# A hybrid mixer and FFN block on one core: the tile of split x is moved by 32 bytes in SBUF

## Chip, cores and metric

The kernel runs on one core of one Trainium2 chip. The time is the device time of one execution in microseconds. Three runs of the kernel before took 1726.85, 1731.55 and 1733.17 us; the median is 1731.55.

## What is computed

One layer of a post-norm trunk, for 256 tokens of 2048 channels, all in float32. `reference.py`, cut down:

```python
def reference(x, ...):
    mix = token_mixing(x, ...)
    x = layer_norm(DEEPNORM_ALPHA * x + mix, ln1_g, ln1_b)
    ffn = conv_ffn(x, ffn_w_up, ffn_conv_w, ffn_conv_b, ffn_w_down)
    return layer_norm(DEEPNORM_ALPHA * x + ffn, ln2_g, ln2_b)

def token_mixing(x, ...):
    proj = x @ w_in + b_in
    fox_qkv, fox_f, sgu_uv, gdn_qkv, gdn_a, gdn_b, gdn_gate, gates = jnp.split(proj, ...)
    y_a = forgetting_attention(fq, fk, fv, jax.nn.log_sigmoid(fox_f))
    y_b = spatial_gating(su, sv, ...)
    y_c = gdn_mixer(gdn_qkv, gdn_a, gdn_b, gdn_gate, ...)
    gt = jax.nn.sigmoid(gates).reshape(bsz, s, N_BRANCH, D_MODEL)
    merged = (gt[:, :, 0] * (y_a @ w_proj_a) + gt[:, :, 1] * (y_b @ w_proj_b)
              + gt[:, :, 2] * (y_c @ w_proj_c))
    return merged @ w_out

def conv_ffn(x, w_up, conv_w, conv_b, w_down):
    h = causal_depthwise_conv(x @ w_up, conv_w) + conv_b
    h_gate, h_val = jnp.split(h, 2, axis=-1)
    return (jax.nn.silu(h_gate) * h_val) @ w_down
```

`w_in` has 2048 x 15384 elements, `w_up` 2048 x 11008, `w_down` 5504 x 2048.

## The kernel before

Nearly all of the work is products of activations with weights that are read once from memory. To keep float32 accuracy with the fast operand type fp32r, each operand is split in a high part (the value rounded to fp32r, written by ACT at L114) and a low part (the rest, by DVE at L115). A product is then three: high times high, high times low, low times high.

`wload` (L117) brings a piece of weights of 512 KB into a tile `raw` by a DMA on SP's queue and splits it into `wh` and `wl`, each [128, 1024]. Four buffers of each rotate. Two functions use them:

- `stream_a` (L128) makes outputs of [128 tokens, 512 channels] for both blocks of tokens. The activations are the resident operand (loaded into the array, 128 x 128), the weights run through with 512 columns. Three products for each block of 128 rows of weights and each block of tokens: L134 (high, high), L135 (high activations, low weights), L136 (low activations, high weights).
- `stream_b` (L162) makes outputs of [128 channels, 256 tokens]. The weights are the resident operand and the activations run through. High and low part of the activations lie side by side in one row of 512 columns, so L178 does two of the three products at once with 512 columns, and L179 the third with the high part alone, 256 columns. For the last block of rows the order of the two is turned (L181, L182).

`stream_b_halves` (L186) is a variant for the first piece of the FFN: it goes block by block of tokens, and each product runs two separate runs of 128 columns through the array (L199, L200).

The tile of activations in `stream_b` is `xhl` (L235) in the first half of the program and `x1hl` (L958) in the FFN: 128 partitions, 16 blocks of 128 channels, each block a row of 512 columns, 256 tokens of the high part and 256 of the low part. Both are one buffer of the pool `hl`. `xhl` is filled at the start from x by `load_x` (transposes on PE at L243, then the split); `x1hl` is filled from the normed result of the mixers by `x1_turn` (L985). The streams of the input projection that make token rows (values, gates) use `xhl` in `stream_a`, through `xh` and `xl` (L256, L259), as the resident operand. The other products of `stream_a` use tiles from other pools: the mixers' outputs (`yah`, `ybh`, `ych` and their low parts), the merged result (`mh`, `ml`) and the FFN's hidden values (`aH`, `aL`).

The order of the program: the gated delta rule's q, k, v by `stream_b` (0 to about 170 us), the attention's q and k by `stream_b` and its values by `stream_a`, the spatial gate's two halves, twelve pieces of gates and branch projections by `stream_a` (to about 880 us), the output projection, layer norm 1, and the FFN in three groups of hidden blocks (16, 16 and 11), each with `stream_b` up and `stream_a` down. The small work of the mixers (attention, delta rule, gating) is cut into steps that generators yield; `tick` (L100) runs one step between two blocks of weights. A list scheduler sets the order within each engine.

Pools are laid out one behind the other in SBUF in the order in which they are opened: const, small, `wraw` (`raw`), `wspl` (`wh`, `wl`), `hl`, `resp` (x, the merged result, the residual), `wk`, then the mixers' slots or the FFN's tiles. Each tile starts at a multiple of 32 bytes. `raw`, `wh`, `wl`, the tile of `hl`, and the large tiles behind it all start 32 bytes past a multiple of 64. Of the tiles that are operands of PE, the constants `ident`, `utri` and `ones` start at a multiple of 64.

Of the kernel before, what the change touches and what calls it, by code (L numbers as in the profile page):

```python
# [44 lines left out]
def trunk_kernel(ctx, tc, x, w_in, b_in, sgu_ln_g, sgu_ln_b, sgu_w, sgu_b, gdn_conv_w, gdn_a_log,  # L45
# [39 lines left out]

# [1 line left out]
    ident = const.tile([P, P], F32, name="ident")  # L87
# [8 lines left out]

# [1 line left out]
    queue = []  # L98

    def tick():  # L100
        """One step of the oldest pending piece of work, between two steps of a weight stream."""
        while queue:
            try:
                next(queue[0])
                return
            except StopIteration:
                queue.pop(0)
# [9 lines left out]
    def wload(src, k0, nk, c0, n, dst=None, low=nc.vector, ahead=150):  # L117
        """Weight rows k0*128.. (nk blocks), columns c0..c0+n: list over blocks of (high, low) views."""
        with tc.high_priority(offset=ahead):
            raw = wraw.tile([P, 1024], F32, tag="raw", name=nm("raw"))  # L120
            rv = raw[:, 0:nk * n].rearrange("p (k n) -> p k n", n=n)
            nc.sync.dma_start(rv, src[k0 * P:(k0 + nk) * P, c0:c0 + n].rearrange("(k p) n -> p k n", p=P))
            hh, ll = dst or (wspl.tile([P, 1024], F32R, tag="wh", name=nm("wh")),
                             wspl.tile([P, 1024], F32R, tag="wl", name=nm("wl")))
            split(hh[:, 0:nk * n], ll[:, 0:nk * n], raw[:, 0:nk * n], low)
        return [(hh[:, j * n:(j + 1) * n], ll[:, j * n:(j + 1) * n]) for j in range(nk)]

    def stream_a(src, nkb, c0, lh, ll, k_off=0, tail=0, spare=(), spare_last=False, done=None, pre=None):  # L128
        """[tokens, 512] outputs for both token blocks; the last tail k blocks go block by block of tokens."""
        accs = [acc(), acc()]  # L130
# [31 lines left out]
    def stream_b(src, c0, n, act, pre=None):  # L162
        """n//128 blocks of [128 channels, (main 256 | low part 256)]."""
        nb = n // P
# [21 lines left out]
    def stream_b_halves(src, c0, act):  # L186
        """As stream_b for 2 blocks, the tokens block by block: [128 channels, (main 2 x 128 | low part 2 x 128)]."""
        accs = [acc() for _ in range(2)]
        ws = []
        for k0 in range(0, KB, 4):  # L190
            ws += wload(src, k0, 4, c0, 256, low=nc.gpsimd)
        av = act.rearrange("p k (u t) -> p k u t", u=2)
        for tb in range(2):
            ts = slice(tb * P, (tb + 1) * P)
            for kb, w in enumerate(ws):
                for i in range(2):
                    a = accs[i].rearrange("p (u t) -> p u t", u=2)[:, :, ts]
                    cs = slice(i * P, (i + 1) * P)
                    nc.tensor.matmul(a, w[0][:, cs], av[:, kb, :, ts], start=kb == 0, stop=False)  # L199
                    nc.tensor.matmul(a, w[1][:, cs], av[:, kb, :, ts], start=False, stop=kb == KB - 1)  # L200
        return accs
# [4 lines left out]
    def rsqrt(dst, src, n):  # L206
        """dst = src ** -0.5 for positive normal src, by Newton steps."""
        t = sm(n)
# [6 lines left out]
    def rsqrt_column(dst, src):  # L215
        """The same for one column; the steps y <- y (y^2 src - 3) leave powers of two to the end."""
        t = sm(1)
# [6 lines left out]
    def rows_to_cols(src_rows, nr, name):  # L224
        """DRAM rows [nr, 128] -> SBUF [128, nr]."""
        r = wk.tile([P, 512], F32, tag="wk", name=nm("rows"))
# [6 lines left out]

# [1 line left out]
    xhl = hl.tile([P, KB, 2 * S], F32R, tag="hl", name="xhl")  # L235

    def transpose_split(dst_h, dst_l, src, kbs):
        """src(kb, tb) [128 tok, 128] -> dst_h/dst_l (kbs) for two blocks at a time."""
        p = mx()
# [21 lines left out]

# [1 line left out]
    mixers = ExitStack()  # L263
# [16 lines left out]
    def small_columns():  # L280
        """Forget gates, decays and betas: cumulative sums by rows, by columns and spread over partitions."""
        wsm = wraw.tile([P, 1024], F32, tag="raw", name="wsm")
        wsv = wsm[:, 0:KB * 24].rearrange("p (k n) -> p k n", n=24)
        nc.sync.dma_start(wsv[:, :, 0:8], w_in[:, O_FF:O_FF + 8].rearrange("(k p) n -> p k n", p=P))
        nc.sync.dma_start(wsv[:, :, 8:24], w_in[:, O_GA:O_GA + 16].rearrange("(k p) n -> p k n", p=P))
        # 24 high and 24 low columns side by side
        wst = wspl.tile([P, 1024], F32R, tag="wh", name="wst")[:, 0:KB * 48].rearrange("p (k u n) -> p k u n", u=2, n=24)
        split(wst[:, :, 0, :], wst[:, :, 1, :], wsv)
        # columns of w_in: 8 forget gates, 8 decays, 8 betas
        bsm = const.tile([48, 1], F32, name="bsm")  # L290
# [32 lines left out]
        nc.scalar.activation(g.beta, pv2[:, :, 16:24], AF.Sigmoid)  # L323
        # softplus(z) = max(z, 0) + log1p(exp(-|z|)); z = -f for the forget gates, a + dt for the decays
        z = const.tile([P, 2, 16], F32, name="z")
# [10 lines left out]
        nc.scalar.activation(e, zn, AF.Exp)  # L336
        # log1p(e) = 2 atanh(e / (2 + e))
        r = col32("r")
# [17 lines left out]
        for _ in range(8):  # L356
            yield
        # rows [16, 256] (forget: whole sequence; decay: per 128 tokens)
        ps = mx()
# [18 lines left out]

# [1 line left out]
    def inv_norm(ss, name):  # L380
        """1 / norm [128 tokens, 2, 8] from sums of squares [128, 16]."""
        nc.vector.tensor_scalar_add(ss, ss, RMS_EPS)
        rn = const.tile([P, 16], F32, name=name)
        rsqrt(rn, ss, 16)
        return rn.rearrange("p (t h) -> p t h", t=2)
# [7 lines left out]
    def gdn_decays():  # L393
        gnat, gbc = g.gnat, g.gbc
        # decays: dt[j, i] = exp(gc_i - gc_j), i >= j;  am[i, j] = exp(gc_i - gc_j), i > j
        dt_ = g.dt = slot("dt").rearrange("p (t h e) -> p t h e", t=2, h=H)
# [8 lines left out]
        for tb in range(2):  # L405
# [5 lines left out]
            yield  # L411
        # decay to the end of the first block
        g.el = const.tile([P, 8], F32, name="el")
# [3 lines left out]
        nc.scalar.activation(g.fw, gnat[:, 1, :], AF.Exp)  # L417
        # decayed queries of the second block: their factors
        nc.scalar.activation(gbc[:, :, P:S], gbc[:, :, P:S], AF.Exp)

    def gdn_keys():
# [17 lines left out]
        nc.vector.tensor_mul(fa, g.fv, rk)  # L439
        # row factor of k @ S in the second block: fa * exp(gc)  # L440
        nc.vector.tensor_mul(g.fw, g.fw, fa[:, 1, :])
        for tb in range(2):
            nc.gpsimd.tensor_mul(am[:, tb], am[:, tb], fa[:, tb, :, None].to_broadcast([P, H, P]))
        yield
        # inverse of (I + am): 32x32 diagonal blocks by elimination, one block per partition
        amv = g.amv = am.rearrange("p t h e -> p (t h) e")
# [22 lines left out]
    def gdn_inverse():  # L469
        amv, td = g.amv, g.td  # L470
        # keys by tokens, first block
        for q in range(2):
# [17 lines left out]
        yield  # L490
        # 32 -> 64
        pm = const.tile([P, 2, 32], F32, name="pm")
# [14 lines left out]
        for q in range(2):  # L507
# [8 lines left out]
            yield  # L516
        # of T itself only the first 64 are needed
        p8 = mx().rearrange("p (m e) -> p m e", e=32)
# [3 lines left out]
        yield  # L522
        # 64 -> 128 (transposed inverse only)
        p2s = []
# [53 lines left out]
    def gdn_blocks():  # L578
# [45 lines left out]
        for q, qs, hs in pair:  # L624
# [5 lines left out]
            yield  # L630
        # tot = rqs * rsqrt(rqs^2 * mean(oraw^2) + eps), rqs = rq / sqrt(head_dim)
        ssq = const.tile([P, 16], F32, name="ssq")
# [16 lines left out]

# [1 line left out]
    yH = [None] * 3  # L651
# [87 lines left out]

# [1 line left out]
    def sgu_norm():  # L741
# [65 lines left out]

# [1 line left out]
    ups = [cpool.tile([P, S + 4], F32, tag=f"up{i}", bufs=1, name=f"up{i}") for i in range(2)]  # L809
# [94 lines left out]

# [1 line left out]
    merged = resp.tile([P, 2, D], F32, tag="res", name="merged")  # L906
# [41 lines left out]

# [1 line left out]
    lng = slot("lng")  # L950
# [6 lines left out]
    st1 = const.tile([P, 2, 4, 6], F32, name="st1")  # L957
    x1hl = hl.tile([P, KB, 2 * S], F32R, tag="hl", name="x1hl")  # L958

    def layer_norm(z, stats, gain, shift, modes, chunk_done=None):  # L960
        """z [128 tokens, 2048] in place, 512 columns at a time; modes: who works on each chunk."""
        mv = sm(2)
# [59 lines left out]

# [1 line left out]
    fp = ctx.enter_context(tc.tile_pool(name="fp", bufs=1))  # L1024
# [107 lines left out]
```

## Time and profile before

| | |
|---|---|
| median of three runs | 1731.55 us (1726.85 to 1733.17) |
| span of the profiled execution | 1727.9 us |
| median less span | 3.65 us |
| PE busy | 1689.7 us, 98% |
| DVE, ACT, POOL busy | 1119.2, 780.9, 262.5 us |
| mean granted TensorE clock | 0.993 |
| DMA | 325.51 MB, mean 188 GB/s |

The span runs from the first to the last instruction of one profiled execution; the times of the runs hold some microseconds more around it. [...]

### The profile page before, as it was taken

The numbers are of one execution on the slowest core, as the hardware profiler recorded it, in microseconds if no ns is written. First come the engines' busy times: TensorE is split into PE (matmuls) and PEld (weight loads), VectorE is DVE, ScalarE is ACT, GpSimd is POOL, SyncE is SP. The second block draws the span as 40 slices with busy tenths as digits, with TensorE's granted clock in tenths as the row PEclk, the third lists the DMA queues.
The fourth block names the chain that finished last, engine by engine and source line by source line (L and its number), as shares of the span: only waits on it lengthen the run. The fifth ranks groups of instructions, "written<-read, shape, count | busy, mean of one in ns | idle before, by whom it ended". The sixth has DMA issues, their size and how long they took to land.

```text
span 1727.9 us, 22873 instructions
## 1 busy us (share of the span) xinstructions
PE 1689.7 (98%) x8738; PEld 1435.5 (83%) x8738; DVE 1119.2 (65%) x1516; ACT 780.9 (45%) x985; POOL 262.5 (15%) x213
## 2 busy tenths in 40 slices
PE   8989999999999999999999999999999999999996
PEld 7877898888888888888888788888888888888885
DVE  5999555577665555555555777775567776567767
ACT  5543444354444444444443355544344544344542
POOL 0259030304230000100100301110001110001102
PEclk9999899999999999999999999999999999999998
DMA  8563646766666666666676476666666665666653
GB/s 239 171 183 97 172 113 196 240 182 173 194 191 206 200 201 206 199 198 200 198 268 213 148 219 183 184 185 195 192 190 185 184 188 191 194 185 194 185 178 112
DMA packets 245249, 325.51 MB, mean 188 GB/s; under 512 B 18844, under 2 KB 159764, under 8 KB 244116
## 3 DMA queue, kind: packets, MB, share of 16 engines
q1 hardware_dynamic: 245140, 324.06, 63.0%
q8 instruction: 68, 1.11, 0.3%
q14 instruction: 41, 0.34, 0.1%
HBM read 321.38 MB, written 2.64 MB: 188 GB/s over the span
## 4 chain that ended last, share of the span: by engine, by line
PE 91%; DVE 6%; issue 1%; DMA 1%; ACT 0%; DVEq 0%; SPq 0%; ACTq 0%
PE acc L178 24%; PE acc L136 16%; PE acc L134 16%; PE acc L135 16%; PE acc L179 12%; PE acc L182 2%; DVE wl L115 1%; DVE cv L832 1%; PE acc L181 1%; DVE z L974 1%; PE mx L243 1%; DVE cv L830 0%; DVE z L973 0%; ACT wh L114 0%; DMA x_sb<-in_x_dram 0%
## 5 line engine op out<-in xcount | busy, mean ns | idle before, releaser
L115 DVE TENSOR_TENSOR wl<-raw,wh 128x1024 fp32r<-128x1024 f32 (+1 forms) x568 | 716.7, 1263 | 494.7 <-ACT wh L114 485.8
L114 ACT ACTIVATE wh<-raw 128x1024 fp32r<-128x1024 f32 x572 | 603.8, 1056 | 686.4 <-PE acc L136 417.2
L178 PE MATMUL acc<-x1hl,wh 128*128 128x512 f32 x1260 | 446.6, 398 | 0.0
L179 PE MATMUL acc<-x1hl,wl 128*128 128x256 f32 x1260 | 354.0, 281 | 0.0
L178 PEld LDWEIGHTS acc<-x1hl,wh 128*128 128x128 f32 x1260 | 236.7, 188 | 56.4
L178 PE MATMUL acc<-xhl,wh 128*128 128x512 f32 x720 | 259.6, 402 | 2.4 <-ACT wh L114 2.4
L179 PEld LDWEIGHTS acc<-x1hl,wl 128*128 128x128 f32 x1260 | 238.1, 189 | 1.7
L134 PE MATMUL acc<-wh,xhl 128*128 128x512 f32 x576 | 226.6, 393 | 0.0
L135 PE MATMUL acc<-wl,xhl 128*128 128x512 f32 x576 | 224.5, 390 | 0.0
L136 PE MATMUL acc<-wh,xhl 128*128 128x512 f32 x576 | 224.4, 390 | 0.0
L179 PE MATMUL acc<-xhl,wl 128*128 128x256 f32 x720 | 205.8, 286 | 7.2 <-DVE wl L115 7.2
L178 PEld LDWEIGHTS acc<-xhl,wh 128*128 128x128 f32 x720 | 137.0, 191 | 33.0 <-ACT wh L114 2.7
L1076 POOL TENSOR_TENSOR cvv<-cvv,cvg 128x256 f32<-128x256 f32 x43 | 56.5, 1332 | 607.3 <-DVE cvv L1047 607.3
L179 PEld LDWEIGHTS acc<-xhl,wl 128*128 128x128 f32 x720 | 137.9, 192 | 11.8 <-DVE wl L115 10.5
L136 PE MATMUL acc<-wh,aL 128*128 128x512 f32 x328 | 127.6, 389 | 0.0
L135 PE MATMUL acc<-wl,aH 128*128 128x512 f32 x328 | 127.6, 389 | 0.0
L134 PE MATMUL acc<-wh,aH 128*128 128x512 f32 x328 | 127.6, 389 | 0.0
L136 PEld LDWEIGHTS acc<-wh,xhl 128*128 128x128 f32 x576 | 108.1, 188 | 22.5
L135 PEld LDWEIGHTS acc<-wl,xhl 128*128 128x128 f32 x576 | 108.2, 188 | 21.9
L134 PEld LDWEIGHTS acc<-wh,xhl 128*128 128x128 f32 x576 | 108.2, 188 | 21.9
L945 POOL TENSOR_TENSOR merged<-merged,wk 128x512 f32<-128x512 f32 x16 | 28.3, 1787 | 362.9 <-DVE wk L943 362.9
L135 PEld LDWEIGHTS acc<-wl,aH 128*128 128x128 f32 x328 | 61.6, 188 | 12.9
(352 smaller groups left out, 1898.3 us busy)
## 6 DMA issues: line engine op xcount, KB each, us to landing
raw<-in_w_in_dram SPq DMA_DIRECT2D x240, 512.0 KB, 3.7
raw<-in_ffn_w_up_dram SPq DMA_DIRECT2D x172, 512.0 KB, 3.9
raw<-in_ffn_w_down_dram SPq DMA_DIRECT2D x84, 512.0 KB, 4.3
raw<-in_w_out_dram SPq DMA_DIRECT2D x32, 512.0 KB, 4.4
raw<-in_w_proj_a_dram SPq DMA_DIRECT2D x16, 512.0 KB, 3.6
raw<-in_w_proj_b_dram SPq DMA_DIRECT2D x16, 512.0 KB, 3.6
raw<-in_w_proj_c_dram SPq DMA_DIRECT2D x16, 512.0 KB, 3.7
wk<-in_b_in_dram SPq DMA_DIRECT2D x18, 256.0 KB, 3.9
```

Of the source, the lines that this page charges most:

```text
L114: nc.scalar.activation(dst_h, src, AF.Copy)
L115: low.tensor_sub(dst_l, src, dst_h.bitcast(F32))
L134: nc.tensor.matmul(a, lh(kb, tb), w[0], start=kb == 0, stop=False)
L135: nc.tensor.matmul(a, lh(kb, tb), w[1], start=False, stop=False)
L136: nc.tensor.matmul(a, ll(kb, tb), w[0], start=False, stop=kb == nkb - 1)
L178: nc.tensor.matmul(a, wh[:, cs], act[:, kb, :], start=kb == 0, stop=False)
L179: nc.tensor.matmul(a[:, 0:S], wl[:, cs], act[:, kb, 0:S], start=False, stop=False)
L181: nc.tensor.matmul(a[:, 0:S], wl[:, cs], act[:, kb, 0:S], start=False, stop=False)
L182: nc.tensor.matmul(a, wh[:, cs], act[:, kb, :], start=False, stop=True)
L243: nc.tensor.transpose(pv[:, i, tb * P:(tb + 1) * P], src(kb, tb), ident)
L945: nc.gpsimd.tensor_add(merged[:, tb, cs], merged[:, tb, cs], gts[tb])
L1076: nc.gpsimd.tensor_mul(cv, cv, cvg[i])
```

## The change

The tile of the pool `hl` gets 16 more float32 elements per partition (64 bytes), and the data begin 8 elements (32 bytes) into it. This holds for `xhl` and for `x1hl`. The rest of the diff takes away comments.

```diff
-    xhl = hl.tile([P, KB, 2 * S], F32R, tag="hl", name="xhl")
+
+    def hl_tile(name):
+
+        t = hl.tile([P, KB * 2 * S + 16], F32R, tag="hl", name=name)
+        return t[:, 8:8 + KB * 2 * S].rearrange("p (k s) -> p k s", s=2 * S)
+
+    xhl = hl_tile("xhl")
...
-    x1hl = hl.tile([P, KB, 2 * S], F32R, tag="hl", name="x1hl")
+    x1hl = hl_tile("x1hl")
```

The changed lines push the lines behind them down by five (L178 to L182 stand ahead of it and keep their numbers). The engines' instructions and their order are the same in both programs.

## Rows read from the trace of the kernel before

**Rows 1.** The page, parts 1 and 4: busy time of the engines, and the chain

```profile
PE 1689.7 (98%) x8738; PEld 1435.5 (83%) x8738; DVE 1119.2 (65%) x1516; ACT 780.9 (45%) x985; POOL 262.5 (15%) x213
...
PE 91%; DVE 6%; issue 1%; DMA 1%; ACT 0%; DVEq 0%; SPq 0%; ACTq 0%
PE acc L178 24%; PE acc L136 16%; PE acc L134 16%; PE acc L135 16%; PE acc L179 12%; PE acc L182 2%; DVE wl L115 1%; DVE cv L832 1%; PE acc L181 1%; DVE z L974 1%; PE mx L243 1%; DVE cv L830 0%; DVE z L973 0%; ACT wh L114 0%; DMA x_sb<-in_x_dram 0%
```

**Rows 2.** Groups by line: count, busy us and mean ns, then idle us before them

```profile
L178 PE MATMUL acc<-x1hl,wh 128*128 128x512 f32 x1260 | 446.6, 398 | 0.0
L179 PE MATMUL acc<-x1hl,wl 128*128 128x256 f32 x1260 | 354.0, 281 | 0.0
L178 PE MATMUL acc<-xhl,wh 128*128 128x512 f32 x720 | 259.6, 402 | 2.4 <-ACT wh L114 2.4
...
L134 PE MATMUL acc<-wh,xhl 128*128 128x512 f32 x576 | 226.6, 393 | 0.0
...
L179 PE MATMUL acc<-xhl,wl 128*128 128x256 f32 x720 | 205.8, 286 | 7.2 <-DVE wl L115 7.2
...
L134 PEld LDWEIGHTS acc<-wh,xhl 128*128 128x128 f32 x576 | 108.2, 188 | 21.9
...
L182 PE MATMUL acc<-x1hl,wh 128*128 128x512 f32 x84 | 31.5, 396 | 0.0
...
L182 PE MATMUL acc<-xhl,wh 128*128 128x512 f32 x48 | 17.9, 396 | 0.0
```

**Rows 3.** PE in order of time in the FFN's `stream_b`: start us, length us

```profile
1100.04 0.40 PE L178 MATMUL acc<-x1hl,wh 128*128 128x512 f32 x1
1100.27 0.28 PE L179 MATMUL acc<-x1hl,wl 128*128 128x256 f32 x1
1100.38 0.40 PE L178 MATMUL acc<-x1hl,wh 128*128 128x512 f32 x1
...
1102.87 0.40 PE L178 MATMUL acc<-x1hl,wh 128*128 128x512 f32 x1
```

**Rows 4.** The same view in `stream_a` on `xhl`

```profile
599.62 0.39 PE L136 MATMUL acc<-wh,xhl 128*128 128x512 f32 x1
599.84 0.39 PE L134 MATMUL acc<-wh,xhl 128*128 128x512 f32 x1
...
601.66 0.39 PE L136 MATMUL acc<-wh,xhl 128*128 128x512 f32 x1
```

**Rows 5.** The same view in `stream_b_halves`

```profile
986.75 0.28 PE L200 MATMUL acc<-x1hl,wl 128*128 128x256 f32 x1
986.87 0.28 PE L199 MATMUL acc<-x1hl,wh 128*128 128x256 f32 x1
...
987.95 0.28 PE L200 MATMUL acc<-x1hl,wl 128*128 128x256 f32 x1
```

**Rows 6.** The same view at L305; then its line: ns min/median/max

```profile
26.38 2.94 PE L305 MATMUL mx<-xhl,wst 128*48 128x512 f32 x12
...
L305 PE MATMUL mx<-xhl,wst x16: 387/396/399, 26.4 to 30.3; 128*48 128x512 f32 x16
```

**Rows 7.** The same two views at L686 (float32, not fp32r)

```profile
349.93 1.03 PE L686 MATMUL mx<-fkT,fqT 128*128 128x256 f32 x4
...
L686 PE MATMUL mx<-fkT,fqT x16: 379/379/382, 349.9 to 371.7; 128*128 128x256 f32 x16
```

**Rows 8.** Float32 products of 128 columns in order of time

```profile
65.56 0.39 PE L360 MATMUL mx<-utri,glog 128*16 128x128 f32 x2
65.78 0.38 PE L361 MATMUL mx<-utri,glog 128*16 128x128 f32 x2
...
241.57 0.39 PE L628 MATMUL mx<-gw,dt 128*128 128x128 f32 x2
...
242.47 0.39 PE L628 MATMUL mx<-gw,dt 128*128 128x128 f32 x2
```

**Rows 9.** Stretches: us, then busy us of each engine, granted clock, DMA share, GB/s

```profile
0.00:150.00 150.00, 138.66 (x797) 117.99 (x797) 128.73 (x220) 78.75 (x110) 54.95 (x66) 1.00 0.64 184
445.00:880.00 435.00, 435.00 (x1958) 360.83 (x1957) 243.41 (x227) 191.17 (x202) 46.81 (x29) 1.00 0.68 204
986.00:989.00 3.00, 3.00 (x27) 3.00 (x26) 2.75 (x11) 0.93 (x2) 0.04 (x1) 1.00 0.00 0
1003.00:1172.00 169.00, 169.00 (x961) 146.89 (x960) 122.57 (x195) 84.91 (x121) 18.62 (x14) 1.00 0.65 189
```

**Rows 10.** The same view, the instructions of L178 alone

```profile
0.00:150.00 150.00, 110.86 (x309) 58.52 (x309) 1.00 0.64 184
```

## The prediction, made blind

> **What bounds the kernel now.** I read the page's shares and its chain first. TensorE is busy 98% of the 1727.9 us and carries 91% of the chain that ended last; DVE has 6%, DMA 1% [rows 1]. So the time is, to a few per cent, the sum of the steps from one product to the next on PE. That sum can only change through the number of steps or the length of one. The groups by line say which they are [rows 2]: the products of `stream_b`, which read the moved tile as the operand that runs through the array (L178 and L179: 1260 pairs on `x1hl`, 720 on `xhl`; L181 and L182: 84 and 48 more of each), and those of `stream_a` (L134 to L136), of which 576 of each line load the moved tile as the resident operand and let the weights run. The mean durations in these groups (398 and 281 ns) overlap, so they aren't the steps. Those must be taken from start to start in order of time.
>
> In order of time, between 1100.04 and 1102.87 us there are eight pairs of a 512-column and a 256-column product of `stream_b`, with no idle time between them [rows 3]: 2.83 us / 8 = 353.75 ns a pair, some 236 and 118. [...]
>
> [...]
>
> **The change part by part.** (1) The instructions, their order and their waits are the same on every engine; nothing is added or removed: 0 us. (2) The addresses. The built program puts the tile at byte 73312 of each partition, 1145 x 64 + 32; the change's data begin at 73344, 1146 x 64. The sixteen extra elements are 64 bytes, so all that is allocated behind (x_sb, wk, the slots, the FFN's tiles) moves by 64 and stays where it was within 64 bytes; the weight tiles, allocated ahead of it, stay at 32 past a multiple. (3) Those later tiles are operands of DVE, ACT and the resident operands of the other `stream_a` products. They keep their place within 64 bytes, so I price them at 0. If a DVE or ACT operation did change by a few ns, PE's slack would cover it: in all, PE stood idle 7.2 us for DVE before L179 and 2.4 us for ACT before L178 [rows 2]. Where DVE itself carries the chain (layer norms, the first stage) it has 6% of it [rows 1]; one per cent on that would be 1 us.
>
> (4) x as the running operand: 1344 + 768 = 2112 pairs, and 64 + 64 products of `stream_b_halves`. The trace has no fp32r product whose operand starts at a multiple of 64, so the price is bounded. *Below*: 0. [...] 13.3 ns x 2112 = 28.1 us, and 6.7 x 128 = 0.9: 29.0 us. [...]
>
> What would be late next: in the FFN's first group PE is busy all of the 169 us, DVE 122.6 and ACT 84.9, DMA 0.65 at 189 GB/s [rows 9], so 4% less PE time there needs some 197 GB/s, which the gates' stretch shows (204). In the first 150 us it isn't so: PE is idle 11.3 us, DVE busy 128.7. 309 pairs lie there [rows 10], 4.1 us of the gain; I count half. Left: **27 us**.
>
> (5) x as the resident operand, 1728 products of `stream_a`: the load of 188 ns [rows 2] lies beside the 226.7 of the product before; a shorter load frees nothing. 0 us, above bounded by 1728 x 6.7 = 11.6, below by the second rival.
>
> The sum: 1727.9 - 27 = 1700.9 us of span. The profiled span is 3.65 below the median of the runs, 1731.55; by that median the prediction is **1704.5 us**.
>
> [...]
>
> **The rivals.** *The start address is of no account* (0.32): the 13.3 ns belong to fp32r itself, say to the change of the resident operand. [...] Time 1731.5, give or take 4.
>
> *The two reads fall out of step* (0.14): today x and weights lie at the same place within 64 bytes. Afterwards the weights run 32 bytes off the resident x in `stream_a`, and the clean 226.7 could take on the 236 that x shows as the running operand: 9.3 ns x 1728 = 16.1 us, with nothing gained in `stream_b`: 1747.6. It decides if `stream_b` gives back less than 16.1 / 2112 = 7.6 ns a pair. For it: L305 and L178 show that the step depends on more than columns. [...]
>
> [...]
>
> That the change doesn't move the data is excluded by the addresses.
>
> **How the numbers follow.** Forecast with its ends (gains of 9 to 56 us): 0.52. No effect: 0.32. Slower: 0.14, and 0.02 for what I don't see. About 0.5% (8.7 us) is what a measurement of this kernel can tell from no change. Faster 0.53, same 0.32, slower 0.15. The range, 1675 to 1740, takes in the far end of the gain, the case of no effect with its spread, and the mild half of the slower one; if the forecast's case holds, 1685 to 1718.
>
> **What would show it.** Right: the pair at L178/L179 of the old numbering near 340 ns, the halves near 113, `stream_a` still 226.7, loads still 188, the FFN's first group some 6 us shorter. No effect: pair 353 to 354. Out of step: steps over 230 in `stream_a` on `xhl`, 226.7 on the slots' tiles. The prediction is wrong in its size if the 512-column steps alone fall (the 256 ones may be held at 118 by their loads): some 7 ns a pair, 14 us. It is wrong in its reason if PE's steps stay and DVE or ACT rows change instead.

## The result, and the profile after

| | before | after |
|---|---|---|
| median of the runs compared | 1730.6 us (1726.85 to 1733.17, 4 runs) | 1744.91 us (1743.08 to 1747.22, 4 runs) |
| span of the profiled execution | 1727.9 us | 1741.3 us |
| mean granted TensorE clock | 0.993 | 0.992 |

The changed kernel is **slower by 0.85%**: ratio 1.0085, 95% interval 1.007 to 1.0101. The forecast was 1704.5 us; 1744.91 lies 4.9 us above the upper end of the range.

The page after, parts 1 and 4 (as [rows 1]):

```profile
PE 1703.2 (98%) x8738; PEld 1437.5 (83%) x8738; DVE 1118.3 (64%) x1516; ACT 781.2 (45%) x985; POOL 262.9 (15%) x213
...
PE 91%; DVE 6%; issue 1%; DMA 1%; ACT 0%; DVEq 0%; SPq 0%; ACTq 0%
PE acc L178 23%; PE acc L134 16%; PE acc L136 16%; PE acc L135 16%; PE acc L179 12%; PE acc L182 2%; DVE wl L115 1%; DVE cv L837 1%; PE acc L181 1%; PE mx L248 1%; DVE z L979 0%; PE acc L199 0%; PE acc L200 0%; DVE cv L835 0%; DMA raw<-in_w_in_dram 0%
```

PE does the same 8738 products and is busy 1703.2 - 1689.7 = 13.5 us longer; the span grew by 13.4. DVE, ACT and POOL kept their time, and the chain its shares. The loss lies in PE's steps, and no other engine has a part in it.

The groups by line after (as [rows 2]):

```profile
L178 PE MATMUL acc<-x1hl,wh 128*128 128x512 f32 x1260 | 439.2, 391 | 0.0
L179 PE MATMUL acc<-x1hl,wl 128*128 128x256 f32 x1260 | 355.1, 282 | 0.0
...
L178 PE MATMUL acc<-xhl,wh 128*128 128x512 f32 x720 | 257.5, 397 | 2.2 <-ACT wh L114 2.2
...
L134 PE MATMUL acc<-wh,xhl 128*128 128x512 f32 x576 | 230.0, 399 | 0.0
...
L179 PE MATMUL acc<-xhl,wl 128*128 128x256 f32 x720 | 206.7, 288 | 7.6 <-DVE wl L115 7.6
...
L134 PEld LDWEIGHTS acc<-wh,xhl 128*128 128x128 f32 x576 | 108.3, 188 | 25.2
```

The records say which way each group went: L178's are 5 to 7 ns shorter (398 to 391, 402 to 397), L134's 6 longer (393 to 399). The load of the resident operand takes 188 ns as before, so a longer load is not what one sees. The idle time before L178 and L179 is as it was.

PE in order of time after, in the FFN's `stream_b` (as [rows 3]):

```profile
1099.80 0.39 PE L178 MATMUL acc<-x1hl,wh 128*128 128x512 f32 x1
1100.03 0.28 PE L179 MATMUL acc<-x1hl,wl 128*128 128x256 f32 x1
1100.15 0.39 PE L178 MATMUL acc<-x1hl,wh 128*128 128x512 f32 x1
...
1102.57 0.39 PE L178 MATMUL acc<-x1hl,wh 128*128 128x512 f32 x1
```

Eight pairs take 2.77 us, 346.3 ns each instead of 353.75. It is the 512-column step that is shorter. The same view in `stream_a` on `xhl` (as [rows 4]):

```profile
599.58 0.40 PE L134 MATMUL acc<-wh,xhl 128*128 128x512 f32 x1
599.81 0.40 PE L135 MATMUL acc<-wl,xhl 128*128 128x512 f32 x1
...
601.68 0.40 PE L134 MATMUL acc<-wh,xhl 128*128 128x512 f32 x1
```

Nine steps take 2.10 us: 233.3 ns, where the nine steps of rows 4 take 2.04 us, 226.7 ns each. Not only `xhl` pays. The records of L134 tile by tile (how many; ns least/median/most; first and last start in us), two rows of before and then four of after:

```profile
L134 PE MATMUL acc<-wh,xhl x576: 387/389/580, 299.1 to 878.1; 128*128 128x512 f32 x192
L134 PE MATMUL acc<-wh,aH x328: 387/389/396, 1172.4 to 1710.8; 128*128 128x512 f32 x164
```

```profile
L134 PE MATMUL acc<-wh,xhl x576: 392/396/582, 297.6 to 889.9; 128*128 128x512 f32 x192
L134 PE MATMUL acc<-wh,aH x328: 391/394/398, 1184.5 to 1724.4; 128*128 128x512 f32 x164
L134 PE MATMUL acc<-wh,yah x64: 393/397/398, 518.4 to 629.7; 128*128 128x512 f32 x64
L134 PE MATMUL acc<-sh,mh x16: 388/389/395, 979.9 to 991.3; 128*128 128x512 f32 x16
```

Before, every one of these medians was 389. A record of 389 goes with a step of 227 ns, one of 394 to 397 with 232 to 234. The change leaves `aH` and `yah` where they were within 64 bytes: they lie in pools behind `hl` and went up by 64 bytes as a whole. The last row points to the rest: there the weights (`sh`) were split into a spare tile of such a pool, so that **both operands moved by 64 bytes together, and the step stayed**.

The sum, from the steps from start to start over the whole trace (means over all pairs or all successive products of one kind): 1344 FFN pairs from 352.7 to 347.1 ns give back 7.5 us; 768 pairs on `xhl` from 350.6 to 347.4 give 2.4; 1728 products of `stream_a` on `xhl` from 227.1 to 233.2 cost 10.7; 1896 others (without the 96 on spare tiles) from 226.7 to 233.3 cost 12.5. Net 13.3 us, of 13.4 in the span.

Two stretches show both signs at once, here and below: 445 to 880 us (gates and branch projections, `stream_a`) and 1030 to 1160 us (nothing but FFN pairs). The more products (the x behind PE's time) in the stretch, the shorter the step. Before, then after; columns as [rows 9]:

```profile
445.00:880.00 435.00, 435.00 (x1958) 360.83 (x1957) 243.41 (x227) 191.17 (x202) 46.81 (x29) 1.00 0.68 204
1030.00:1160.00 130.00, 130.00 (x738) 112.85 (x737) 92.80 (x147) 63.77 (x91) 15.94 (x12) 1.00 0.64 187
```

```profile
445.00:880.00 435.00, 435.00 (x1906) 351.60 (x1905) 236.43 (x221) 186.34 (x197) 46.87 (x29) 1.00 0.62 195
1030.00:1160.00 130.00, 130.00 (x751) 114.95 (x750) 95.69 (x153) 65.03 (x94) 15.98 (x12) 1.00 0.63 190
```

1958 products became 1906 in the one and 738 became 751 in the other. The granted clock is 1.00 in all four.

### The profile page after: what moved, and what is told of

Same layout as the page of the kernel before. It is cut to its first block, busy times and chain, and to the rows that moved or that the text cites. A ratio compares the mean times of both kernels' runs of the same rounds, so it can differ in the third digit from the quotient of the medians.

```text
span 1741.3 us, 22873 instructions
## 1 busy us (share of the span) xinstructions
PE 1703.2 (98%) x8738; PEld 1437.5 (83%) x8738; DVE 1118.3 (64%) x1516; ACT 781.2 (45%) x985; POOL 262.9 (15%) x213
## 4 chain that ended last, share of the span: by engine, by line
PE 91%; DVE 6%; issue 1%; DMA 1%; ACT 0%; DVEq 0%; SPq 0%; ACTq 0%
PE acc L178 23%; PE acc L134 16%; PE acc L136 16%; PE acc L135 16%; PE acc L179 12%; PE acc L182 2%; DVE wl L115 1%; DVE cv L837 1%; PE acc L181 1%; PE mx L248 1%; DVE z L979 0%; PE acc L199 0%; PE acc L200 0%; DVE cv L835 0%; DMA raw<-in_w_in_dram 0%
## 5 line engine op out<-in xcount | busy, mean ns | idle before, releaser
L178 PE MATMUL acc<-x1hl,wh 128*128 128x512 f32 x1260 | 439.2, 391 | 0.0
L179 PE MATMUL acc<-x1hl,wl 128*128 128x256 f32 x1260 | 355.1, 282 | 0.0
L178 PEld LDWEIGHTS acc<-x1hl,wh 128*128 128x128 f32 x1260 | 236.4, 188 | 48.8
L178 PE MATMUL acc<-xhl,wh 128*128 128x512 f32 x720 | 257.5, 397 | 2.2 <-ACT wh L114 2.2
L179 PEld LDWEIGHTS acc<-x1hl,wl 128*128 128x128 f32 x1260 | 237.9, 189 | 1.8
L134 PE MATMUL acc<-wh,xhl 128*128 128x512 f32 x576 | 230.0, 399 | 0.0
L135 PE MATMUL acc<-wl,xhl 128*128 128x512 f32 x576 | 228.0, 396 | 0.0
L136 PE MATMUL acc<-wh,xhl 128*128 128x512 f32 x576 | 227.7, 395 | 0.0
L179 PE MATMUL acc<-xhl,wl 128*128 128x256 f32 x720 | 206.7, 288 | 7.6 <-DVE wl L115 7.6
L178 PEld LDWEIGHTS acc<-xhl,wh 128*128 128x128 f32 x720 | 137.0, 191 | 30.0 <-ACT wh L114 2.5
L179 PEld LDWEIGHTS acc<-xhl,wl 128*128 128x128 f32 x720 | 137.8, 192 | 12.2 <-DVE wl L115 10.9
L136 PEld LDWEIGHTS acc<-wh,xhl 128*128 128x128 f32 x576 | 108.2, 188 | 25.9
L136 PE MATMUL acc<-wh,aL 128*128 128x512 f32 x328 | 129.6, 395 | 0.0
L135 PE MATMUL acc<-wl,aH 128*128 128x512 f32 x328 | 129.6, 395 | 0.0
L134 PE MATMUL acc<-wh,aH 128*128 128x512 f32 x328 | 129.6, 395 | 0.0
L134 PEld LDWEIGHTS acc<-wh,xhl 128*128 128x128 f32 x576 | 108.3, 188 | 25.2
L135 PEld LDWEIGHTS acc<-wl,xhl 128*128 128x128 f32 x576 | 108.3, 188 | 25.0
L135 PEld LDWEIGHTS acc<-wl,aH 128*128 128x128 f32 x328 | 61.6, 188 | 14.9
```

The lines of the kernel that those rows point to most:

```text
L134: nc.tensor.matmul(a, lh(kb, tb), w[0], start=kb == 0, stop=False)
L135: nc.tensor.matmul(a, lh(kb, tb), w[1], start=False, stop=False)
L136: nc.tensor.matmul(a, ll(kb, tb), w[0], start=False, stop=kb == nkb - 1)
L178: nc.tensor.matmul(a, wh[:, cs], act[:, kb, :], start=kb == 0, stop=False)
L179: nc.tensor.matmul(a[:, 0:S], wl[:, cs], act[:, kb, 0:S], start=False, stop=False)
```

## The experiments

All start from the kernel before. The theory that stood at the end, R: the step depends on where PE's two operands lie **against each other**, not on where each lies. Its rivals are named in each text. The first kernels and the scan change the tile of `hl` in three numbers: the offset of `xhl`, that of `x1hl`, and the padding, by which all later tiles move.

```diff
-    xhl = hl.tile([P, KB, 2 * S], F32R, tag="hl", name="xhl")
+    def hl_tile(name, at):
+        t = hl.tile([P, KB * 2 * S + PAD], F32R, tag="hl", name=name)
+        return t[:, at:at + KB * 2 * S].rearrange("p (k s) -> p k s", s=2 * S)
+    xhl = hl_tile("xhl", A)
...
-    x1hl = hl.tile([P, KB, 2 * S], F32R, tag="hl", name="x1hl")
+    x1hl = hl_tile("x1hl", B)
```

**Only the later tiles move** (A 0, B 0, PAD 16 elements: 64 bytes).

> The tile of x stays where it was (offset 0) and only the 64 bytes of padding are kept, so only the tiles allocated behind it move, by 64 bytes. Theory R (what counts is the place of the running operand against that of the resident one, within 128 bytes: a step of stream_a is 227 ns where both are the same and 233 where they differ, and stream_b's pair is 353 where both are the same and 346 where x lies 32 bytes off): stream_a on yah, ybh, ych, mh and aH steps at 233, on xhl at 227, stream_b's pair at 353; 1992 steps, less the 96 of the spare pieces, cost 6.6 ns each, 12.5 us: 1743. Theory X (the moved x alone explains it, the later tiles' steps changed with it through something else): nothing but the before time, 1731, and 227 everywhere in stream_a.

Measured: 1743.04 us against 1730.9 of the kernel before on the same chip, ratio 1.0075 [1.006, 1.009]. The two stretches, and two rows of L134:

```profile
445.00:880.00 435.00, 435.00 (x1942) 357.95 (x1941) 239.71 (x224) 189.97 (x200) 46.86 (x29) 1.00 0.68 201
1030.00:1160.00 130.00, 130.00 (x739) 112.88 (x738) 93.35 (x151) 64.99 (x94) 13.30 (x10) 1.00 0.64 187
```

```profile
L134 PE MATMUL acc<-wh,xhl x576: 387/389/579, 301.1 to 883.5; 128*128 128x512 f32 x192
L134 PE MATMUL acc<-wh,aH x328: 394/394/397, 1181.0 to 1725.1; 128*128 128x512 f32 x164
```

With x untouched, the pairs are as before (352.2 ns) and so is `stream_a` on `xhl` (227.2), but every product whose activations lie in a later tile takes 233. This term, which the forecast priced at nothing, costs 12.1 us by itself; what the moved x costs (10.7) and gives back (9.9) nearly cancel. The theory that puts the loss on the moved x falls; R holds, at its number.

**The 32 bytes as in the change, the later tiles by 128** (A 8, B 8, PAD 32).

> The data of x and x1 begin 32 bytes into the tile as in the change, but the padding is 128 bytes, so the tiles behind it keep their place within 128. Theory R: stream_b's pair 346, stream_a on xhl 233, stream_a on all other tiles 227: 2112 x 7 = 14.8 us gained, 1728 x 6.6 = 11.4 lost, 1727 to 1728. Theory X: as the change, 1745, with 233 in all of stream_a.

Measured: 1742.76 us, ratio 1.0082 [1.0059, 1.0105]. A miss by 15 us:

```profile
L134 PE MATMUL acc<-wh,aH x328: 390/395/398, 1183.2 to 1723.0; 128*128 128x512 f32 x164
L134 PE MATMUL acc<-wh,yah x64: 390/393/404, 518.5 to 629.6; 128*128 128x512 f32 x64
```

I had expected that a shift of 128 bytes is none; the later tiles' steps are 232 to 233 ns there too. The place repeats over more than 128 bytes, if it repeats.

**Everything behind the constants moves by 32 bytes together**, so that all streamed operands start at a multiple of 64 and keep their places against each other.

```diff
-    st2 = const.tile([P, 2, 4, 6], F32, name="st2")
+    st2 = const.tile([P, 56], F32, name="st2")[:, 0:48].rearrange("p (t c s) -> p t c s", t=2, c=4)
```

> Everything from the small pool on (weights, x, all tiles behind) moves by 32 bytes together, by 32 bytes more behind the last constant; all operands of the streams then start at multiples of 128. Theory R (places against each other): nothing changes, 353 and 227, 1731. Theory A (absolute place: a start at a multiple of 64 saves a part of the 13.3 ns): stream_a near 220 and the pair below 346, below 1710.

Measured: 1730.39 us against 1730.9, ratio 0.9993 [0.998, 1.0006], and the two stretches of the kernel before to within one product:

```profile
445.00:880.00 435.00, 435.00 (x1957) 360.87 (x1956) 243.54 (x227) 192.01 (x203) 46.82 (x29) 1.00 0.68 203
1030.00:1160.00 130.00, 130.00 (x739) 112.93 (x738) 92.81 (x147) 63.64 (x91) 15.96 (x12) 1.00 0.64 187
```

This is the change that theory A asks for, a start at a multiple of 64 for the running x, and it gives nothing. **At this shift the absolute place is of no account.**

**Only x1 by 32 bytes, later tiles by 128** (A 0, B 8, PAD 32).

> Only x1hl begins 32 bytes in, xhl at offset 0, padding of 128 bytes. x1hl is only ever the running operand. Theory R: the FFN's pairs at 346, the pairs on xhl at 353, stream_a at 227 throughout: 1344 pairs x 7 ns = 9.4 us faster than before, 1721 to 1722. Theory X: between 1731 and 1745.

Measured: 1735.99 us (1731.61 to 1739.43), ratio 1.0033 [1.0021, 1.0045]; 1721 to 1722 had been expected. The pairs came as expected (347.1 ns, x751 in the second stretch), `xhl` kept 227.1, and the later tiles again took 232 to 233: the same miss. By the steps the later tiles cost 11.6 us and the pairs give back 7.5, so 4.1 of the 5.1 us between the medians are accounted for. The profiled run (span 1730.1 us, granted clock 0.991) is among the two shortest of ten; the longest has 1737.7 us at 0.989, and what it had longer is open.

**A scan of the three numbers**, one run each, against 1729.51 us of the kernel before. Nineteen runs of the kernel before on one chip go from 1728.16 to 1735.98 us, so kernels with a single run, here and below, are told apart by their steps and not by their times. In bytes (offset of `xhl`, of `x1hl`, padding): 16, 64, 256; then 256, 128, 288; then 64, 16, 96; then 192, 96, 192.

> xhl begins 16 bytes into its tile, x1hl 64, the tiles behind move by 256. Theory R (the place of the running operand against the resident one, now known to repeat over more than 128 bytes). Period 256: stream_a on yah, mh, aH is back at 227. Period 512: it stays at 232 to 234. Theory U (each meeting of the two reads costs one unit of 16 columns, 6.7 ns): all mean steps are columns plus a whole number of units: 512-column steps of stream_a 220, 226.7 or 233.3, pairs of stream_b 340, 346.7 or 353.3. Theory S (the place of the single operand in its own 512 bytes, not against the other): x1hl 64 bytes further changes its pair, and the tiles behind, at a place of their own, need not return at 256.

> xhl begins 256 bytes into its tile, x1hl 128, the tiles behind move by 288. Theory R, period 256: stream_a on xhl 227 and its pairs 353 as before; the tiles behind as at 32, 233; period 512: xhl in stream_a over 230. Theory U: whole units throughout.

> xhl begins 64 bytes into its tile, x1hl 16, the tiles behind move by 96. Theory R: stream_a on xhl at 233, as the tiles behind had it at 64; the pair on x1hl at 16 is open, 346 if any difference will do, 353 if 16 is too little. Theory U: whole units throughout.

> xhl begins 192 bytes into its tile, x1hl 96, the tiles behind move by 192. Theory R: stream_a over 230 on all tiles, pairs near 346. Theory U: whole units throughout; any place with 220 in stream_a or 340 in a pair would give a kernel faster than both.

Measured: 1729.19, 1737.77, 1745.15 and 1737.86 us. The first has its later tiles 256 bytes up, and there all is as before, while `xhl` (16 bytes up) has a step of 229.1. In the second it is `xhl` that went up by 256, and it is the one with 227.1. L134 on `aH` in the first, on `xhl` in the second:

```profile
L134 PE MATMUL acc<-wh,aH x328: 389/389/400, 1175.0 to 1710.4; 128*128 128x512 f32 x164
L134 PE MATMUL acc<-wh,xhl x576: 387/389/577, 297.8 to 880.2; 128*128 128x512 f32 x192
```

So **the place repeats every 256 bytes** in these runs. The steps that the scan gave, with those of the kernels above and below (mean steps from start to start over the trace, the three lines of `stream_a` together; the place is that of the running operand less that of the resident one, modulo 256 bytes):

| place | `stream_a`, ns a product | FFN pair, ns | pair on `xhl`, ns |
|---|---|---|---|
| 0 | 226.7 to 227.2 | 352.2 to 352.7 | 349.7 to 350.7 |
| 16 | 227.1 | 347.2 | 348.6 |
| 32 | not run | 347.1 to 347.2 | 347.3 to 347.4 |
| 64 | 228.9 to 229.0; 233.1 in the FFN's third group | 349.2 | 350.8 |
| 96 | not run | 350.3 | not run |
| 128 | 232.3 to 233.3 | 350.9 | not run |
| 160 | 234.1 to 234.3 | not run | not run |
| 192 | 233.3 | not run | 352.8 |
| 224 | 233.2 to 233.3 | 352.6 | not run |
| 240 | 229.1 | not run | 351.9 |

The fourth kernel missed its text on both counts: over 230 in `stream_a` on all tiles and pairs near 346 were expected, and the rows for 64 and 96 have other numbers. Theory U falls with means such as 229.1 at 240, which are no whole number of units (its 6.7 ns for 16 columns agrees with an estimate from rows 4 and 5, steps of 226.7 ns for 512 columns and 120 for 256: (226.7 - 120) / 256 = 0.417 ns a column), and a theory by which only whole steps of 32 or 64 bytes count falls with 347.2 at 16. The place has a sign: 16 and 240 differ in `stream_a` (227.1 and 229.1 ns). And the two functions want different places: equal ones give `stream_a` its shortest step, while the pairs of `stream_b` are shortest at 16 to 32 and, at equal places, among the longest.

**Other operands as the cause.** `raw` (what the DMA writes and ACT and DVE read) gets 16 elements more, so that its four buffers lie at four different places:

```diff
-            raw = wraw.tile([P, 1024], F32, tag="raw", name=nm("raw"))
+            raw = wraw.tile([P, 1040], F32, tag="raw", name=nm("raw"))
```

> Only the four raw buffers, which PE never reads, get 64 bytes of padding each: they lie at 0, 64, 128 and 192 within 256, and all that comes behind moves by 256 together. Theory R (two reads of PE meet): nothing changes, 353 and 227, 1729 to 1731. Theory E (PE's read meets the writes and reads of DMA, ACT and DVE, whose operands are raw): the steps change with the raw buffer in use, above 230 in a part of stream_a.

Measured: 1730.43 us against 1730.55; all steps as before, x1958 and x738 in the two stretches. The place of `raw` has no part in it.

**A better version.** The table says: leave `xhl` and all later tiles where `stream_a` is best, and move `x1hl` alone, which no `stream_a` uses (A 0, B 8, PAD 64: 256 bytes).

> xhl at 0, x1hl 32 bytes in, padding of 256 bytes, so that only the FFN's running operand lies off its resident one and all of stream_a keeps its place within 256. Theory R with period 256: stream_a 226.7 to 227 throughout, the FFN's pairs 347.1, the others as before: 1344 x 5.6 ns = 7.5 us faster than before, 1723 to 1724. Theory X (a tile behind that moves at all costs stream_a its step): 1735 or more.

Measured: 1722.37 us (1720.47 to 1723.28) against 1730.55, ratio 0.9944 [0.9929, 0.9959]; span 1720.7. It is faster than both kernels. Its page's first part and the two stretches:

```profile
PE 1682.1 (98%) x8738; PEld 1436.1 (83%) x8738; DVE 1118.9 (65%) x1516; ACT 781.0 (45%) x985; POOL 262.7 (15%) x213
```

```profile
445.00:880.00 435.00, 435.00 (x1958) 360.86 (x1958) 243.56 (x227) 190.53 (x202) 46.84 (x29) 1.00 0.68 204
1030.00:1160.00 130.00, 130.00 (x751) 114.92 (x750) 94.30 (x150) 65.02 (x95) 15.98 (x12) 1.00 0.65 190
```

The first stretch is that of the kernel before, the second that of the change: 1344 pairs x 5.5 ns = 7.4 us, and the span is 7.2 shorter.

**The sign once more** (offset of `xhl` 240 bytes, of `x1hl` 224, padding 256).

> xhl begins 240 bytes into its tile (16 short of the period), x1hl 224 (32 short), the tiles behind move by 256. Theory R: stream_a on the tiles behind 226.7 to 227; xhl in stream_a near 229, if the sign of the difference has no part, as at 16; x1hl's pair near 347, as at 32. If the sign has a part, one of them is at 227 or less, or at 353.

Measured: 1731.76 us against 1730.55. `stream_a` on `xhl` has 227.1 ns with the resident operand 240 bytes up, where 16 bytes up gave 229.1; the FFN pair has 352.6. So the sign has a part.

**Which product of a triple pays?** First `wl`'s four buffers are put at four places, `wh` stays:

```diff
-                             wspl.tile([P, 1024], F32R, tag="wl", name=nm("wl")))
+                             wspl.tile([P, 1040], F32R, tag="wl", name=nm("wl")))
```

> Only the four buffers of the low weights get 64 bytes of padding each: they lie at 0, 64, 128 and 192 within 256 against wh, x and the tiles behind, which move by 256 together. Theory R: in stream_a only the step in which wl runs through (L135) changes, with the buffer: 227 on one, 230 to 234 on the others; L134 and L136 stay at 227. In stream_b wl is the resident operand of L179, loaded while L178 runs: pairs 353 on one buffer and 347 to 351 on the others, and the change lies in L178's step, not in L179's. Theory S (place of a single operand): L134 and L136, whose operands do not move, change as well, or L135 does not.

Measured: 1736.66 us against 1730.55. By `wl`'s place (0, 64, 128, 192) the mean step of the triple L134 to L136 is 227.7, 232.1, 232.6 and 229.9 ns. I had expected L135, the only one that reads `wl`, to change alone; at 64 the three are 231.2, 232.2 and 232.9. The expectation is missed: a product's step depends on its neighbours' operands too. In the FFN's pairs the change lies in L178's step, as expected (231.8 ns in the mean instead of 235.8), but on the buffer at 0, too, where 353 was expected, the pair takes 348.0.

Then only `aL` begins 64 bytes off, the resident operand of L136 in the FFN's down products:

```diff
-        aL = actp.tile([P, 16, S], F32R, tag="aL", name=nm("aL"))
+        aL = actp.tile([P, 16 * S + 64], F32R, tag="aL", name=nm("aL"))
+        aL = aL[:, 16:16 + 16 * S].rearrange("p (k s) -> p k s", s=S)
```

> Only aL, the low part of the FFN's hidden values, begins 64 bytes off (a resident operand of L136 alone; the tiles keep multiples of 256 otherwise). Theory N (what runs meets the load of the next product): L135 runs while aL is loaded, so its step alone goes to 233, L134 and L136 stay at 227: 328 x 6.4 ns, 2 us. Theory O (a product's own two operands): L136 alone goes to 233. Theory J (a product pays for a running operand that begins at another place than the last one did): nothing changes, all at 227.

Measured: 1734.7 us against 1729.98. PE in order of time in a down stretch:

```profile
1249.83 0.39 PE L134 MATMUL acc<-wh,aH 128*128 128x512 f32 x1
1250.06 0.39 PE L135 MATMUL acc<-wl,aH 128*128 128x512 f32 x1
1250.28 0.40 PE L136 MATMUL acc<-wh,aL 128*128 128x512 f32 x1
...
1251.91 0.39 PE L134 MATMUL acc<-wh,aH 128*128 128x512 f32 x1
```

Three triples take 2.08 us, 693 ns each instead of 680. Over the trace the steps of L134, L135 and L136 are 228.4, 229.3 and 235.6: 13 ns more a triple, 4.3 us over 328 of them, of 4.7 measured. Two thirds lie on L136, the only product that has `aL` as its resident operand; the rest on its neighbours. So none of the three theories has these numbers; O is nearest. All other tiles kept their steps.

Last, `wl` everywhere 64 bytes off `wh`, and `aL` too; a few FFN constants change pools so that the rest keeps its places against each other:

```diff
-                             wspl.tile([P, 1024], F32R, tag="wl", name=nm("wl")))
+                             wspl.tile([P, 1088], F32R, tag="wl", name=nm("wl"))[:, 16:1040])
...
+        aL = actp.tile([P, 16 * S + 64], F32R, tag="aL", name=nm("aL"))
+        aL = aL[:, 16:16 + 16 * S].rearrange("p (k s) -> p k s", s=S)
```

> All low weights lie 64 bytes off the high ones, and so does aL; four constants of the FFN move to the FFN's pool to make room. In the FFN's down products each running operand meets the load of one at its own place (wl with aL, wh with aH), but successive running operands begin at two places. Theory N: 227 in all three steps there; on xhl, yah and mh, whose low parts have not moved, L135 alone at 229 (it lay 64 behind its resident in another run). Theory O: L135 and L136 off 227 in the down products, L134 at 227. Theory J: all three above 227 everywhere, alike on aH and on xhl.

Measured: 1742.72 us against 1729.98. On `aH` and `aL` the three steps are 232.0, 231.5 and 230.6, on `xhl` 231.4, 232.2 and 232.4: no line is spared. That is what J's text says, but J failed in the kernel before this one; N and O fail here. None of the three has the numbers of both kernels. FFN pairs: 346.9.

**What stays open** is the mechanism. The runs show that the places of the operands against each other change the steps, modulo 256 bytes (226.7 to 234.3 ns a product in `stream_a`), and that successive products are coupled (228.4 and 229.3 ns beside 235.6 where `aL` alone had moved). They don't show by what, and the table doesn't follow from any rule that I tried. Nor is the place all of it: at 64 (the fourth kernel of the scan) the FFN's first and third group have `aH` and `aL` in the same buffers, and a product takes 228.9 ns in the one and 233.1 in the other. The first and second group have the same mean there but share it out otherwise over L134 to L136 (229.0, 231.7, 226.1 and 225.9, 229.2, 231.7), so the step of a single line says little of whose operand costs it.

## Why the prediction was wrong, by its steps

**What bounds the kernel: right.** The time is the sum of PE's steps, in number unchanged. PE's busy time grew by 13.5 us and the span by 13.4. The sum went wrong in three terms, worth 40.3 of the 40.4 us between 1704.5 and 1744.91: the gain of part (4) was put 17.1 us too high, and the costs in parts (3) and (5), 12.5 and 10.7 us, at nothing. The 3.65 us from the profiled span to the median hold after as well (3.6): 1.7 to 1.8 lie around the span in the runs on record, and the rest is that the profiled execution was a short one.

**Parts (1) and (2), order and addresses: right.** The addresses also held the answer: the later tiles move by 64 bytes.

**Part (3), the later tiles at 0: wrong.** Without this cost, the other two terms as measured would have left the time within 1 us of the kernel before. "They keep their place within 64 bytes" assumed that only the place within 64 counts. The place counts within 256, and 64 bytes cost 6.6 ns on each of 1896 products, 12.5 us; the kernel that moves those tiles alone loses 0.75% [0.6, 0.9]. Rows could have bounded this: all the `stream_a` products of the kernel before had equal places, so none showed what another place costs, and 9.3 ns on 1896 more products belonged in the bounds, as they were used for `xhl`.

**Part (4), x as the running operand: right in sign, wrong in reason and in size.** The pairs did fall, by 5.6 ns in the FFN and 3.2 on `xhl`, 9.9 us in all instead of 28.1 (27 with the halves and the first stage); the 512-column step alone carries it, as the text named for its being wrong in size ("some 7 ns a pair"; eight pairs in order of time show 7.4, the whole trace less). The reason, a start at a multiple of 64, fell with the kernel whose streams all have one and whose time didn't change (0.9993 [0.998, 1.0006]). No run shows the prices in the sum, 13.3 ns a pair and 6.7 ns a half, nor the gain of 56 us at the far end of the range; in their place the runs showed 5.6 and 3.2 ns a pair and some 2 a half. The halves went from 120 (rows 5) to some 118, not to 113:

```profile
1002.03 0.28 PE L199 MATMUL acc<-x1hl,wh 128*128 128x256 f32 x1
1002.15 0.28 PE L200 MATMUL acc<-x1hl,wl 128*128 128x256 f32 x1
...
1002.97 0.28 PE L199 MATMUL acc<-x1hl,wh 128*128 128x256 f32 x1
```

Eight steps in 0.94 us are 117.5 ns.

**Part (5), x as the resident operand at 0: wrong.** The argument, that a load of 188 ns lies hidden beside a step of 226.7, is true of the load's length and misses that the place of the resident operand can lengthen the step: 6.2 ns x 1728 = 10.7 us. Nor does a run show the 6.7 ns a product of its upper bound; 6.2 were lost. In the kernel that moves the later tiles alone, too, moving only resident operands took the step from 227 to 233 ns with the running ones untouched.

**The rivals.** *No account* (0.32) was right about the start address and wrong about the time, since it is the places against each other that moved. *Out of step* (0.14) had the right idea (products of 512 columns had three steps before: 226.7 ns in rows 4, (2.94 - 0.396) / 11 = 231 at L305 in rows 6, some 236 at L178) and a near time, 1747.6, by luck, since three errors nearly cancel: it put 16.1 us on `xhl` alone, where 10.7 were measured, and nothing on the other tiles ("226.7 on the slots' tiles"), where 12.5 were; and it gave `stream_b` no gain, where 9.9 came. At equal places `stream_b` takes 352.7 ns a pair, while `stream_a` has its shortest step there: the two functions want different places.

## What to carry to other kernels

Padding ahead of a tile moves every tile behind it. List all operands of PE whose place against their partner changes, not only the one in the diff, and count the products on each. Where PE is the bound, pad in multiples of 256 bytes, so that the rest keeps its places (226.7 to 227.2 ns in `stream_a` here), and then shift one operand of one loop at a time; 32 bytes on a tile that only `stream_b` uses gave 0.56% [0.41, 0.71] here.

## What the runs showed of the hardware that I had not expected

In these kernels an fp32r product's step depends on the place of its operands against each other modulo 256 bytes: 226.7 to 234.3 ns for 512 columns with the weights running, 347.1 to 352.8 for the pair with the activations running. Moving all of them together by 32 bytes changes nothing (0.9993 [0.998, 1.0006]). One operand out of place lengthens the neighbours' steps as well (228.4 and 229.3 beside 235.6, where all three had some 227). The load's own record shows none of this; L134's stays at 188 ns.
